# Branch products as seven products of quarters: what a two-block kernel's TensorE and its transfers make of it

## The chip, the cores and the metric

The kernel runs on one core of a Trainium2 chip. The metric is the device time of one execution in microseconds (us). Three runs of the kernel before took 1120.37, 1123.80 and 1120.04 us; their median is 1120.37.

## The reference

The input is one sequence of 512 tokens and 1024 features in float32. Two blocks follow each other. The first is a norm with modulation, a projection to 6144 columns, a pooling branch and a linear recurrence in chunks, and an output projection with a residual. The second has four branches of width 512 (a gated spatial mix, a sparse attention, a short convolution, an attention with forgetting), each with its own output product and its own gates, and these are what the change is about:

```python
h = rms_norm_2(x, norm_g)                      # 512 x 1024
proj = h @ w_in                                # its last 4096 columns are "gates"
ys = jnp.stack([y_a, y_b, y_c, y_d], axis=0)   # 4 x 512 tokens x 512
branch_d = jnp.einsum('nbsw,nwd->bsnd', ys, w_branch)      # 4 products 512x512 by 512x1024
g = jax.nn.sigmoid(gates.reshape(bsz, s, N_BRANCH, d))     # 4 products 512x1024 by 1024x1024
merged = jnp.sum(g * branch_d, axis=2)
return x + merged @ w_out                      # then a last norm
```

## The kernel before

**Products in three parts.** Every float32 operand is split into a high part and a rest, both in the fp32r format; `x w` is then high by high, high by rest and rest by high, three matmuls of 128x128 by 128x512. ScalarE copies the high part of a weight block into `whi` (L302), VectorE subtracts it for `wlo` (L303). There are three pairs of these buffers (WB) and splits run two products ahead (LA); `wget` hands out a pair and lets `pump` write the next ones. Activations are split by `split` (VectorE's line is L355), and one line, L329, issues every matmul.

**Weights.** The host lays all weights out as blocks ("raws") of 128 x 2048, 1024 KB, in the order in which they are used. SP loads them one after the other into a raw buffer as soon as one is free (`dma_raw`, L247; `used` frees one). There are three raw buffers; ahead of the gate stage three more are made, each of four 128x512 working tiles (`add_buf`). There are 54 working tiles ("slots") in all, which hold whatever else is live.

**The gate stage.** The branches come in the order 0, 2, 3, 1. Per branch the 512x1024 by 1024x1024 gate product is computed as seven products of quarters (`strassen_gate`, PRODUCTS), each of two items of 12 matmuls. The weights' quarters are combined where they lie: when a product's weights are split, `add_quarter` has POOL issue a transfer that adds the next quarter from DRAM to the one in the buffer (L261, ADDED: four sums of two halves of 512 KB per branch). Between and behind them stand the branch products (`wb_items`): for each half of the columns two loads of two row blocks, each by four blocks of 128 tokens, in three parts: 96 matmuls a branch. Their activations y (four tiles of 128x512 a branch) stay in slots from where a branch is computed. Their results are multiplied by the gate's sigmoid (L1769) and added to the sum over branches (L1774), both on VectorE:

```python
V.tensor_mul(s.f, s.f, hold["b"][t][:])
...
V.tensor_add(mg[t, hf].f, mg[t, hf].f, s.f)
```

`merged_T` then transposes the sum for the output product `w2`, which follows. What sets the order around the change: each engine runs its list as written by the items' order; SP's queue is in the order of the blocks, and POOL's in the order in which `add_quarter` is called.

**Other places that the change touches.** At the start, VectorE reduces the modulation's weights (`ttr`) in eight steps, each followed by 21 matmuls. In the first block `u_evac` builds window sums for the pooling by shift-and-add steps on POOL (L914), `spread` takes a squared tile, splits it and multiplies by a ones matrix to sum over partitions, `gate_item` reads the modulation's gate weights out of raw buffers (blocks `adg`), and `rstd` with `after1` and `norm_T` makes the two norms between the blocks (L1148, L1152, L1159). L1364 scales an attention's probabilities ahead of their transposes (L1395). XD keeps the residual in DRAM during the second block.

## Time and profile before

| | |
|---|---|
| median of three runs | 1120.37 us |
| the profiled execution's own time | 1121.16 us |
| its span, first to last instruction | 1119.4 us |
| mean granted TensorE clock | 0.998 |
| TensorE matmuls, busy | 1093.8 us, 98% of the span, 5189 |
| VectorE, ScalarE, POOL busy | 785.0, 636.8, 107.0 us |
| DMA | 139.54 MB, mean 125 GB/s |

The page comes from one execution. A busy time is the sum of an engine's instructions; matmuls are pipelined and their ends modelled, so the share of TensorE says that it rarely stands, not that it runs at its best. PEclk is the granted clock in parts of full speed (1.0 is 2.4 GHz, 0.5 is 1.2 GHz). The DMA share is the mean over the 16 DMA engines of the time that their packets took; as packets of one engine can lie over one another, a short stretch can read above 1. A chain of waits lists, going back from the last instruction, what each step had to wait for.

### The profile page before, as it was taken

Reading aid. Unit: us, or ns where it says so; the run is one execution under the profiler, and the core shown is the slowest. Engines: PE = TensorE matmul, PEld = TensorE weight load, DVE = VectorE, ACT = ScalarE, POOL = GpSimd, SP = SyncE. Lnnn points to the kernel's source line nnn. Section 1 sums busy time; section 2 is a strip of 40 time slices with the busy share of each in tenths; the row PEclk is TensorE's granted clock in tenths of the full one; section 3 lists DMA queues with packets and bytes.
Section 4 is the critical chain, followed back from the end, with each engine's and each line's share of the span. In section 5 each row is a group of like instructions: output and inputs, shape, how many; then the busy total and the mean of one; then the engine's idle time right before and its main releaser. Section 6 shows DMA issues by size and latency. Waiting matters only on the chain.

```text
span 1119.4 us, 14194 instructions
## 1 busy us (share of the span) xinstructions
PE 1093.8 (98%) x5189; PEld 904.7 (81%) x5189; DVE 785.0 (70%) x1586; ACT 636.8 (57%) x1025; POOL 107.0 (10%) x121
## 2 busy tenths in 40 slices
PE   6999999999999999999999999999999999999997
PEld 4788888888878888788887888888888888888885
DVE  7978788764779645889797846686655657565745
ACT  6595487955478464554246545754664554536513
POOL 1330210100520000000000000000111210122000
PEclk9999999999999999999999999999999999999999
DMA  9734223232222253232322222121586676768202
GB/s 326 285 132 164 80 92 135 76 113 76 76 76 76 96 203 116 95 113 104 122 76 76 85 85 81 71 76 57 169 207 177 173 205 160 188 151 220 101 1 75
DMA packets 39827, 139.54 MB, mean 125 GB/s; under 512 B 4551, under 2 KB 4807, under 8 KB 29901
## 3 DMA queue, kind: packets, MB, share of 16 engines
q1 hardware_dynamic: 32268, 120.81, 30.6%
q0 software_dynamic: 6912, 16.78, 8.7%
q10 hardware_dynamic: 576, 1.05, 0.3%
q8 instruction: 40, 0.66, 0.2%
q14 instruction: 31, 0.25, 0.1%
HBM read 134.42 MB, written 4.20 MB: 124 GB/s over the span
## 4 chain that ended last, share of the span: by engine, by line
PE 85%; DVE 5%; DMA 3%; ACT 3%; issue 2%; POOL 2%; SPq 0%; POOLq 0%; ACTq 0%
PE bank L329 83%; DMA slot<-in_adw_dram 2%; ACT slot L108 1%; PE bank L1395 1%; POOL slot L914 1%; ACT whi L302 1%; ACT L108 1%; POOL slot L913 1%; DMA raw<-in_wts_dram 1%; DVE slot L487 1%; DMA slot<-in_x_dram 1%; DVE slot L355 0%; DVE slot L1148 0%; DVE slot L1159 0%; DVE wlo L303 0%
## 5 line engine op out<-in xcount | busy, mean ns | idle before, releaser
L303 DVE TENSOR_TENSOR wlo<-raw,whi 128x1024 fp32r<-128x1024 f32 (+1 forms) x160 | 194.2, 1214 | 132.6 <-ACT whi L302 123.7
L302 ACT ACTIVATE whi<-raw 128x1024 fp32r<-128x1024 f32 (+1 forms) x160 | 168.1, 1051 | 202.2 <-PE bank L329 170.0
L329 PE MATMUL bank<-HH,whi 128*128 128x512 f32 x704 | 272.3, 397 | 2.4 <-ACT HH L108 2.1
L329 PE MATMUL bank<-HH,wlo 128*128 128x512 f32 x704 | 268.4, 391 | 0.0
L329 PE MATMUL bank<-HL,whi 128*128 128x512 f32 x704 | 267.3, 391 | 0.0
L329 PE MATMUL bank<-whi,slot 128*128 128x512 f32 x688 | 218.1, 392 | 0.0
L108 ACT ACTIVATE slot<-bank 128x512 f32<-128x512 f32 (+7 forms) x286 | 133.1, 495 | 55.5 <-PE bank L329 25.3
L108 ACT ACTIVATE slot<-slot 128x512 fp32r<-128x512 f32 (+4 forms) x199 | 112.3, 593 | 92.0 <-DVE slot L1930 19.2
L329 PEld LDWEIGHTS bank<-HH,whi 128*128 128x128 f32 x704 | 132.1, 188 | 31.8 <-ACT HH L108 5.5
L329 PEld LDWEIGHTS bank<-HH,wlo 128*128 128x128 f32 x704 | 132.5, 188 | 28.0
L329 PEld LDWEIGHTS bank<-HL,whi 128*128 128x128 f32 x704 | 132.6, 188 | 26.3
L329 PEld LDWEIGHTS bank<-whi,slot 128*128 128x128 f32 x688 | 129.1, 188 | 28.8 <-ACT slot L108 1.7
L329 PE MATMUL bank<-slot,slot 128*128 128x128 f32 (+5 forms) x754 | 132.4, 319 | 3.4 <-ACT slot L108 3.4
L329 PE MATMUL bank<-wlo,slot 128*128 128x512 f32 x336 | 130.9, 389 | 0.0
L329 PEld LDWEIGHTS bank<-slot,slot 128*128 128x128 f32 (+2 forms) x754 | 109.4, 186 | 18.2 <-issue 4.4
L108 ACT ACT_TABLE_LOAD x84 | 107.8, 1283 | 3.2 <-PEq L2069 0.7
L329 PE MATMUL bank<-whi,HH 128*128 128x512 f32 x248 | 97.8, 394 | 0.7 <-ACT slot L108 0.5
L329 PE MATMUL bank<-whi,HL 128*128 128x512 f32 x248 | 96.3, 391 | 1.3 <-DVE small L1152 1.3
L329 PE MATMUL bank<-wlo,HH 128*128 128x512 f32 x248 | 96.7, 390 | 0.0
L329 PEld LDWEIGHTS bank<-wlo,slot 128*128 128x128 f32 x336 | 63.1, 188 | 12.7
L261 POOL DMA_DIRECT2D slot<-in_wts_dram x28 | 24.5, 936 | 448.8 <-DMA slot<-in_wts_dram 395.7
L302 ACT ACTIVATE whi<-slot 128x512 fp32r<-128x512 f32 x61 | 38.5, 631 | 45.9 <-PE bank L329 35.2
(236 smaller groups left out, 1192.8 us busy)
## 6 DMA issues: line engine op xcount, KB each, us to landing
raw<-in_wts_dram SPq DMA_DIRECT2D x77, 1024.0 KB, 4.8
slot<-in_wts_dram SPq DMA_DIRECT2D x44, 256.0 KB, 4.8
slot<-in_adw_dram SPq DMA_DIRECT2D x32, 256.0 KB, 6.4
raw<-in_wts_dram POOLq DMA_DIRECT2D x16, 512.0 KB, 5.4
slot<-in_wts_dram POOLq DMA_DIRECT2D x28, 256.0 KB, 5.1
slot<-in_x_dram SPq DMA_DIRECT2D x16, 256.0 KB, 4.0
raw<-in_wts_dram SPq DMA_DIRECT2D x8, 448.0 KB, 5.8
slot<-in_rows_dram SPq DMA_DIRECT2D x11, 256.0 KB, 3.9
```

Source lines behind the costliest of these rows:

```text
L108: return A.activation(o, i, func, **kw)
L261: G.dma_start(b.at(c, w), wts[r_from, :, c:c + w], accum_op=ALU.add)
L302: A.activation(whi[s][:, c:c + n], b.at(o + c, n), AF.Copy)
L303: V.tensor_sub(wlo[s][:, c:c + n], b.at(o + c, n), whi[s][:, c:c + n])
L329: T.matmul(o, l, r, start=start, stop=stop, **kw)
L487: V.tensor_tensor_reduce(junk[i % 2].f, ada[k][i].f, cb[i % 2].f, 1.0, 0.0, ALU.mult, ALU.add, mds[k][:, i:i + 1])
L913: G.tensor_copy(d.f[:, 0:sh], src.f[:, 0:sh])
L914: G.tensor_add(d.f[:, sh:512], src.f[:, sh:512], src.f[:, 0:512 - sh])
L1395: T.transpose(tb[:, cs], P[u1].f[:, cs], IDENT)
```

## The change

**Branch products.** W of a branch (512 x 1024) and y (512 x 512) are cut into quarters, and seven products of quarters of 12 matmuls give what eight would: 84 matmuls a branch. The weights come in three blocks of two quarters, a, b and c, of 1024 KB each; four sums are added by transfers when the blocks have been loaded, a fifth after the third product has been split. Quarters b and c hold a second copy, so seven blocks a branch are loaded for gates and branch products where six were. The adds are no longer issued at once but put on a list (`later`) and issued two items later. The branch products now stand behind all seven gate products.

**y in DRAM.** Each tile of y is written to a DRAM tile YD when a branch has computed it (`keep`, 16 writes of 256 KB) and read back early in the branch's gate products (`y_steps`), where its quarters are split and its four sums formed by VectorE, one step with each item.

**Sums over branches.** In the second and third branch the sum over branches is done by transfers from slot to slot that add (16 of 256 KB), issued by POOL; in the last branch by VectorE.

**From the call's first try.** The gate weights `adg` are loaded into slots four items ahead; two constants are loaded by ScalarE's queue at the start; five more matmuls (WARM) stand behind the first transposes; one reduction goes earlier, copies and one scaling move between VectorE and ScalarE; pooling windows 8 and 16 take one running sum on VectorE and one subtraction; `spread` is handed a split made ahead; the norms multiply by rows that were scaled by -0.5 beforehand and have one VectorE step less; the transposes of the next tokens are written into the products of the current ones; the last norm writes into slots of its own.

```diff
-        pairs += [[f"B{n}_11"], [f"B{n}_21"], [f"B{n}_22"], [f"B{n}_12"], half(n, 1), half(n, 0)]
+        pairs += [[f"B{n}_11"], [f"B{n}_21"], [f"B{n}_22"], [f"B{n}_12"], [f"W{n}_a"], [f"W{n}_b"], [f"W{n}_c"]]
...
+PRODUCTS_W = ((1, "a", 0), (5, "b", 1), (6, "a", 1), (3, "c", 0), (7, "b", 0), (2, "c", 1), (4, "a", 1))
+ADDED_W = (("a", 1, "b", 0), ("b", 0, "c", 0), ("b", 1, "b", 0), ("a", 1, "a", 0))
...
     def dma_raw():
+        while ws["dma"] < len(raws) and raws[ws["dma"]][0][0].startswith("ad"):
+            ws["dma"] += 1
...
-        for o, r_from in to_add.pop(r, ()):
-            add_quarter(r, o, r_from)
+        for args in to_add.pop(r, ()):
+            later.append((ws["next"] + 2, args))
+        name = raws[r][0][0]
+        if name[0] == "W":
+            n = name[1]
+            later.extend((ws["next"] + 2, (r, h * 1024, quarter[f"{n}_{q}"], g * 1024))
+                         for t, h, q, g in ADDED_W if t == name[-1])
...
+            if name[0:2] == "W6":
+                add_quarter(r, o, quarter[f"{name[3]}_c"], 1024)
...
     def wget(name, ahead=LA):
+        while later and later[0][0] <= i:
+            add_quarter(*later.pop(0)[1])
         pump(i + ahead)
...
-    def spread(b, w, src, keep=False):
-        h, l = get(), get()
-        split(h.r, l.r, src.f)
+    def spread(b, w, hl):
+        h, l = hl
...
+            if w > 4:
+                on, d = get(), get()
+                G.memset(on.f, 1.0)
+                V.tensor_tensor_scan(d.f, on.f, u.f, 0.0, op0=ALU.mult, op1=ALU.add)
+                V.tensor_copy(on.f[:, 0:w], d.f[:, 0:w])
+                V.tensor_sub(on.f[:, w:512], d.f[:, w:512], d.f[:, 0:512 - w])
...
-        V.scalar_tensor_tensor(u, r, -0.5, r, op0=ALU.mult, op1=ALU.mult)
-        V.tensor_mul(u, u, v)
-        V.scalar_tensor_tensor(r, u, 1.5, r, op0=ALU.add, op1=ALU.mult)
+        V.scalar_tensor_tensor(u, r, v, r, op0=ALU.mult, op1=ALU.mult)
+        V.scalar_tensor_tensor(r, u, -3.0, r, op0=ALU.add, op1=ALU.mult)
...
+    def keep(n, k, slot):
+        nc.sync.dma_start(y_block(n, k), slot.f)
+        put(slot)
+        yb.add((n, k))
...
+    def y_steps(n):
+        def load():
+            for k in range(4):
+                y.append(get())
+                nc.sync.dma_start(y[k].f, y_block(n, k))
+        def plain(name, i, j):
+            def f():
+                h, l = q[name] = get(), get()
+                for k in range(2):
+                    dh, dl = (two(x).bitcast(F32R)[:, k] for x in (h, l))
+                    split(dh, dl, part(i, j, k))
...
+        return [load, None, None, plain(1, 0, 0), sums_, sum6, sum3, sum7, plain(2, 0, 1), plain(4, 1, 1), rest]
...
+    def wb_items(n):
+        def out(i, hf, part, banks_, free):
+            for t in range(2):
+                s = sg.pop((2 * i + t, hf))
+                b = banks_[t][:]
+                if part:
+                    u = part[t]
...
+                    else:
+                        V.tensor_sub(u.f, u.f, b)
+                    b = u.f
+                V.tensor_mul(s.f, s.f, b)
...
+                if last:
+                    V.tensor_add(mg[key].f, mg[key].f, s.f)
+                else:
+                    G.dma_start(mg[key].f, s.f, accum_op=ALU.add)
+                put(s)
+                for t in range(2):
+                    for k in range(2):
+                        mm(to[t][:], ah[:, k, ts_], h[:, c], opens and k == 0, False, **go)
+                        mm(to[t][:], ah[:, k, ts_], l[:, c], False, False, **go)
+                        mm(to[t][:], al[:, k, ts_], h[:, c], False, k == 1, **go)
+        items = [item(p) for p, _, _ in PRODUCTS_W]
+        if last:
+            items.insert(6, (None, lambda: merged_T(1, (0, 1)), None))
+            items.append((None, lambda: merged_T(1, (2, 3)), None))
...
-        for p, _ in PRODUCTS[0:6]:
+        for p, _ in PRODUCTS:
             r += product(p)
-        r += wb_items(n, 1)
-        a4 = product(4)
...
-        return r + a4 + wb_items(n, 0)
+        for i, f in enumerate(y_steps(n)):
+            if f:
+                r[i + 1] = both(f, r[i + 1])
+        return r + wb_items(n)
```

**POOL's queue in the gate stage, second branch.** A row is a transfer: its destination, its source and its size; 128x1024 is 512 KB. `in_wts_dram` rows add weights to a raw buffer or to slots that serve as one. Before:

```order
L261 DMA raw_113<-in_wts_dram 128x1024
L261 DMA slot_6499<-in_wts_dram 128x512
L261 DMA raw_113<-in_wts_dram 128x1024 x5
L261 DMA raw_114<-in_wts_dram 128x1024 x2
L261 DMA slot_6595<-in_wts_dram 128x512
L261 DMA slot_6596<-in_wts_dram 128x512
```

After, in the same place, with L1899 the sums over branches (L275 is the line of the weights' adds now):

```order
L275 DMA raw_114<-in_wts_dram 128x1024 x4
L275 DMA slot_6622<-in_wts_dram 128x512
L275 DMA slot_6623<-in_wts_dram 128x512
L275 DMA slot_6624<-in_wts_dram 128x512
L275 DMA slot_6625<-in_wts_dram 128x512
L1899 DMA slot_6771<-slot_7225 128x512
L275 DMA raw_113<-in_wts_dram 128x1024
L1899 DMA slot_6773<-slot_7227 128x512
L275 DMA slot_6533<-in_wts_dram 128x512
L275 DMA slot_6534<-in_wts_dram 128x512
L1899 DMA slot_6678<-slot_7132 128x512
L1899 DMA slot_6680<-slot_7134 128x512
```

The adds of weights for branch products have come in, and the sums over branches stand between them and the next branch's adds.

**VectorE at the branch products of the second branch.** `wlo` rows are weight splits; a row that reads a `bank` takes a matmul's result out of its accumulator. Before, L1769 multiplies by the gate and L1774 adds to the sum over branches:

```order
L1769 TENSOR_TENSOR slot_7104<-slot_7104,bank_65 128x512
L1769 TENSOR_TENSOR slot_7106<-slot_7106,bank_66 128x512
L1774 TENSOR_TENSOR slot_6706<-slot_6706,slot_7104 128x512
L1774 TENSOR_TENSOR slot_6708<-slot_6708,slot_7106 128x512
L303 TENSOR_TENSOR wlo_121<-slot_6554,whi_118 128x512
L1769 TENSOR_TENSOR slot_7035<-slot_7035,bank_64 128x512
```

After, L1883 combines two products and L1887 multiplies by the gate:

```order
L1883 TENSOR_TENSOR slot_7371<-bank_61,slot_7371 128x512
L1887 TENSOR_TENSOR slot_7225<-slot_7225,slot_7371 128x512
L317 TENSOR_TENSOR wlo_119<-slot_6624,whi_116 128x512
L1883 TENSOR_TENSOR span_7373<-bank_62,span_7373 128x512
L317 TENSOR_TENSOR wlo_119<-slot_6625,whi_116 128x512
L1887 TENSOR_TENSOR slot_7227<-slot_7227,span_7373 128x512
```

The additions have left VectorE's list in this branch, and combinations and more splits have come.

**SP's queue where the gate stage's loads begin.** A `raw` row of 128x2048 is one block; blocks in slots go in four rows. Before:

```order
L247 DMA raw_114<-in_wts_dram 128x2048
L247 DMA raw_115<-in_wts_dram 128x1024
L247 DMA raw_113<-in_wts_dram 128x2048
L247 DMA slot_6497<-in_wts_dram 128x512
L247 DMA span_6498<-in_wts_dram 128x512
L247 DMA raw_114<-in_wts_dram 128x2048
L247 DMA slot_6496<-in_wts_dram 128x512
```

After, with L1291 the writes of y and L1820 its reads:

```order
L1291 DMA YD<-slot_5829 128x512
L254 DMA raw_113<-in_wts_dram 128x2048
L1291 DMA YD<-slot_6012 128x512
L254 DMA raw_114<-in_wts_dram 128x1024
L254 DMA slot_6623<-in_wts_dram 128x512
L254 DMA slot_6624<-in_wts_dram 128x512
L254 DMA slot_6531<-in_wts_dram 128x512
L254 DMA raw_115<-in_wts_dram 128x2048
L1291 DMA YD<-slot_6098 128x512
L254 DMA slot_6532<-in_wts_dram 128x512
L1820 DMA slot_6555<-YD 128x512
L1820 DMA span_6553<-YD 128x512
```

The 128x1024 row is the last block of the projections in both. The writes and reads of y share the queue with the blocks.

## Rows read from the trace of the kernel before

**Rows 1.** The page's first part: span, busy time and share of each engine

```profile
span 1119.4 us, 14194 instructions
...
PE 1093.8 (98%) x5189; PEld 904.7 (81%) x5189; DVE 785.0 (70%) x1586; ACT 636.8 (57%) x1025; POOL 107.0 (10%) x121
```

**Rows 2.** Chain of waits, gate stage: start us, us, what, matmuls

```profile
850.35 60.41 PE bank L329 x264
...
1055.47 21.84 PE bank L329 x96
```

**Rows 3.** TensorE's timeline, first gate matmul: start us, us, what

```profile
822.58 0.39 PE L329 MATMUL bank<-whi,HH 128*128 128x512 f32 x1
```

**Rows 4.** TensorE's waits, whole span: us in total, times, longest

```profile
PE bank L1395 <- DVE slot L1364: 2.7, 1, 2.7
PE bank L329 <- DVE slot L355: 2.4, 3, 1.8
...
PE bank L329 <- DVE small L1152: 1.3, 1, 1.3
```

**Rows 5.** Windows: length, engines' busy us (count), PEclk, DMA share, GB/s

```profile
785.00:811.00 26.00, 26.00 (x123) 21.72 (x123) 16.74 (x37) 16.66 (x29) 2.80 (x3) 1.00 0.61 182
811.00:850.00 39.00, 38.99 (x177) 32.01 (x175) 22.42 (x28) 23.13 (x33) 6.01 (x7) 1.00 0.83 205
850.00:910.00 60.00, 59.99 (x264) 49.03 (x263) 34.21 (x46) 30.12 (x45) 12.13 (x14) 1.00 0.71 174
910.00:960.00 50.00, 49.99 (x220) 40.77 (x218) 33.90 (x47) 25.82 (x38) 5.21 (x6) 1.00 0.66 169
960.00:1014.00 54.00, 53.99 (x238) 44.37 (x238) 35.25 (x48) 25.90 (x38) 11.40 (x14) 1.00 0.69 176
1014.00:1042.00 28.00, 27.99 (x123) 22.47 (x122) 16.20 (x21) 16.55 (x25) 4.24 (x5) 1.00 1.00 278
1026.00:1034.00 8.00, 7.99 (x36) 6.22 (x35) 4.38 (x7) 4.56 (x7) 0.09 (x1) 1.00 1.08 251
20.00:40.00 20.00, 19.19 (x81) 14.60 (x80) 19.72 (x49) 10.59 (x15) 5.37 (x4) 1.00 1.04 391
```

**Rows 6.** The page's queues: packets, MB, share of 16 engines over the span

```profile
q1 hardware_dynamic: 32268, 120.81, 30.6%
q0 software_dynamic: 6912, 16.78, 8.7%
```

**Rows 7.** The same queues from 980 to 990 us

```profile
q0 software_dynamic: 560, 1.02, 64.1%
q1 hardware_dynamic: 195, 1.13, 32.8%
```

**Rows 8.** SP queue's timeline: the gate stage's first block is issued

```profile
784.97 0.33 SPq L247 DMA_DIRECT2D raw<-in_wts_dram  x1
```

**Rows 9.** TensorE's timeline in the first block, idle time before in brackets

```profile
324.31 1.08 PE L329 MATMUL bank<-slot,ONES 128*128 128x512 f32 x2 [1.75 <-DVE slot L355]
```

**Rows 10.** The window right behind it

```profile
325.00:329.00 4.00, 3.54 (x9) 2.60 (x10) 4.00 (x12) 2.36 (x4) 0.00 (x0) 0.57 0.00 0
```

**Rows 11.** Groups by form, whole span: busy us, mean ns, idle before

```profile
L685 DVE TENSOR_TENSOR_SCAN slot<-SCANM,slot 128x512 f32<-128x512 f32 x8 | 9.8, 1219 | 2.4 <-ACT slot L108 1.5 <-POOL slot L914 0.9
```

**Rows 12.** TensorE's timeline, two steps of the start

```profile
39.26 1.88 PE L329 MATMUL bank<-HH,whi 128*128 128x512 f32 x7
...
44.37 1.88 PE L329 MATMUL bank<-HH,whi 128*128 128x512 f32 x7
```

**Rows 13.** Groups by form from 811 to 1055 us

```profile
L303 DVE TENSOR_TENSOR wlo<-raw,whi 128x1024 fp32r<-128x1024 f32 x38 | 46.5, 1225 | 47.8 <-ACT whi L302 47.7
...
L1769 DVE TENSOR_TENSOR slot<-slot,bank 128x512 f32<-128x512 f32 x28 | 18.5, 681 | 2.1 <-PE bank L329 2.0
...
L261 POOL DMA_DIRECT2D raw<-in_wts_dram x16 | 13.8, 906 | 100.9 <-DVE wlo L303 66.0 <-DMA raw<-in_wts_dram 35.0
```

**Rows 14.** The page's DMA issues: count, KB each, us to landing

```profile
raw<-in_wts_dram POOLq DMA_DIRECT2D x16, 512.0 KB, 5.4
```

More of the change, by code (lines that the diff above doesn't have):

```diff
@@ L29 @@
 NSPAN = 2
+WARM = 5
 R1 = 1.5
@@ L57, in plan @@
 def plan():
-    def half(n, hf):
-        return [f"wb{n}_{hf}_{j}" for j in range(2)]
     raws = []
@@ L194 @@
                 if q == "12":
-                    for p, src in PRODUCTS[0:6]:
+                    for p, src in PRODUCTS:
                         flat += [(f"P{p}n{n}_{j}", f"{n}_{src}", j * 1024, 1024) for j in range(2)]
-            else:
-                if name[0:2] == "wb" and name[3:] == "_0_0":
-                    p, src = PRODUCTS[6]
-                    flat += [(f"P{p}n{name[2]}_{j}", f"{name[2]}_{src}", j * 1024, 1024) for j in range(2)]
+            elif name[0] == "W":
+                quarter[name[1:]] = r
+                n, q = name[1:].split("_")
+                if q == "c":
+                    flat += [(f"W{p}n{n}", f"{n}_{t}", h * 1024, 1024) for p, t, h in PRODUCTS_W]
+            else:
                 flat.append((name, r, o, w))
@@ L259, in add_quarter @@
         w = width(1024, b)
-        for c in range(o, o + 1024, w):
-            G.dma_start(b.at(c, w), wts[r_from, :, c:c + w], accum_op=ALU.add)
+        for c in range(0, 1024, w):
+            G.dma_start(b.at(o + c, w), wts[r_from, :, o_from + c:o_from + c + w], accum_op=ALU.add)
     def add_buf():
@@ L969, with both, mmf, gate_load @@
     gacc = {}
+    def both(first, item):
+        def mmf():
+            first()
+            item[1]()
+        return (item[0], mmf, item[2])
+    def gate_load(m, part):
+        def load():
+            r = flat[names.index(f"adg{m}{part}")][1]
+            gadw[m, part] = [get() for _ in range(4)]
+            for i, t in enumerate(gadw[m, part]):
+                nc.sync.dma_start(t.f, wts[r, :, i * 512:(i + 1) * 512])
+        return load
+    gadw = {}
     def gate_item(m, part):
         def mmf():
-            raw, r = adaget(f"adg{m}{part}")
+            adaget(f"adg{m}{part}")
             if part == "a":
@@ L976, in mmf @@
             acc = gacc[m]
-            acc_cols(acc.f, [raw[:, i * 512:(i + 1) * 512] for i in range(4)], 4 * "ab".index(part), 8)
-            used(r)
+            tiles = gadw.pop((m, part))
+            acc_cols(acc.f, [t.f for t in tiles], 4 * "ab".index(part), 8)
+            put(*tiles)
             if part == "a":
@@ L1136, in wout_final, with scale_row, rstd @@
             put(*src[k])
-    def rstd(t, scaled, row):
+    def scale_row(row):
+        for h in range(2):
+            act(row[h].f, row[h].f, AF.Copy, scale=-0.5)
+    def rstd(src, to, row):
         ss2, v, r, u = small(2), small(1), small(1), small(1)
@@ L1181, in norm_T @@
             dl = HL[:, 4 * h:4 * h + 4, t * 128:(t + 1) * 128]
-            split(dh, dl, b3)
+            with tc.high_priority():
+                split(dh, dl, b3)
             bput(b)
     presplit(mixH, range(8))
+    scale_row(ROW)
     wout_final("wh", mixH, after1)
@@ new lines, in y_steps, with part, two, load @@
+    def y_steps(n):
+        y, q = [], yq[n] = [], {}
+        def part(i, j, k):
+            return y[2 * j + k].f[:, 256 * i:256 * i + 256]
+        def two(s):
+            return s.f.rearrange("p (k t) -> p k t", t=256)
+        def load():
+            while any((n, k) not in yb for k in range(4)):
+                assert sides
+                step_sides(4)
+            for k in range(4):
[7 more added lines that the diff above has]
+                    split(dh, dl, part(i, j, k))
+            return f
+        def sums_():
+            q[5] = get()
+            for k in range(2):
+                V.tensor_sub(two(q[5])[:, k], part(1, 0, k), part(1, 1, k))
+        def sum6():
+            q[6] = get()
+            for k in range(2):
+                V.tensor_sub(two(q[6])[:, k], two(q[5])[:, k], part(0, 0, k))
+        def sum3():
+            q[3] = get()
+            for k in range(2):
+                V.tensor_add(two(q[3])[:, k], two(q[6])[:, k], part(0, 1, k))
+            q[5] = split_slot(q[5])
+        def sum7():
+            q[7] = get()
+            for k in range(2):
+                V.tensor_sub(two(q[7])[:, k], part(0, 0, k), part(1, 0, k))
+            q[6] = split_slot(q[6])
+        def rest():
+            put(*y)
+            q[3] = split_slot(q[3])
+            q[7] = split_slot(q[7])
+        return [load, None, None, plain(1, 0, 0), sums_, sum6, sum3, sum7, plain(2, 0, 1), plain(4, 1, 1), rest]
```

214 lines of the change are left out of this document (121 added, 93 removed).

## Prediction

> **What bounds the kernel now.** The page's first part has TensorE busy for 98% of a span of 1119.4 us [rows 1]. As the ends of its matmuls are modelled, I turned to the chain of waits. In the gate stage (gates and branch products) the chain is TensorE alone, piece joined to piece: 264 matmuls in 60.41 us, so 0.2288 us each [rows 2]. The stage's first matmul starts at 822.58 [rows 3]; its last is the 48th of the piece that begins at 1055.47, and 48 x 0.2275 us later it is 1066.4 [rows 2]. TensorE's list of waits comes third: no wait in it stands in the gate stage, and what there is elsewhere is a few us [rows 4].
>
> Then I looked at what this change loads more, the 16 DMA engines. In the gate stage they are busy for 0.66 to 1.00 of the time [rows 5], though TensorE never waits for them. The page's queues give prices. q1, the plain transfers, takes 30.6% of 1119.4 us for 120.81 MB, 2.835 us of all engines per MB; q0, the adding transfers, 8.7% for 16.78 MB, 5.80 us per MB [rows 6]. Two checks. From 785 to 1042 the shares times the lengths give 189 us [rows 5]; 32.0 MB of loads and 16.78 MB of adds by these prices give 188. And in ten microseconds where both queues run, q0 has 64.1% and q1 32.8% [rows 7]: together 0.97, so one takes its time from the other. The slack is 28%, no more.
>
> **The change, part by part.**
> 1. Branch products. Before, 2 halves x 2 loads x 2 x 4 row blocks x 3 = 96 matmuls a branch; now 7 products x 2 x 2 x 3 = 84. 48 fewer in all at 0.2288 us: -11.0 us of TensorE's chain.
> 2. What they cost the DMA engines. A quarter or block of 1024 KB is 1.049 MB, 2.97 us as a load; an add of half of it 3.04 us. The stage loads 7 blocks a branch instead of 6: 28 x 2.97 = 83.2 us. Adds of weights go from 8 to 13 a branch (8 for the gates as before, 4 when a, b and c are loaded, 1 after the third product): 52 x 3.04 = 158.1. Reading y back: 16 tiles of 0.262 MB at 0.74: 11.9. The sums over branches: 16 adding transfers from SBUF to SBUF, which the trace lacks. The nearest rows are a plain transfer, 0.74, and an add from DRAM, 1.52 [rows 6]; none excludes the low end, and they too read, add and write, so I take 1.52: 24.3 (low end 11.9). Sum 277.5 us, against 168.7 before (24 loads, 32 adds).
> 3. Which of it must be through before the stage ends. The last add is the one into block a between the third and the seventh product of the last branch, and 3.5 of the 4 blocks of the output weights are issued ahead of it: +10.4, so 288. What is done before the first gate matmul comes off. Before, the first load of the stage goes out at 784.97 [rows 8], and until 822.6 the engines do 26 x 0.61 + 11.6 x 0.83 = 25.5 us of work [rows 5]; all 37.6 us would be the most. The change issues two tiles earlier, and has six buffers as before: I take 30. 258 us are left.
> 4. How fast the engines can go. With work waiting they reached 1.00 over 28 us [rows 5]; 0.83 is the row for 811 to 850, with buffers full. A stretch can read above 1: 1.08 over 8 us, and 1.04 over 20 us at the start, 391 GB/s of plain transfers [rows 5], where 2.835 us per MB is 353. I take 0.97 (ends 0.88 and 1.05): 266 us. After the last add come its split, two products and transposes, some 7 us. The stage then ends at 822.6 + 266 + 7 = 1095.6, where before it ended at 1066.4: +29.2 us. TensorE alone would end it at 1055.4. So the 11.0 us are not seen: TensorE waits for splits, these for adds.
> 5. New waits. ScalarE's copies of y wait for its reload, issued three half-products ahead (8 us), and behind them on ScalarE stand the next weight splits; on the POOL queue the sums wait for VectorE's multiplies, and the next branch's adds stand behind them. Both are inside the 0.97 while the DMA engines are the limit. Where TensorE waits, its clock can drop: after 1.75 us of waiting [rows 9] the granted clock is 0.57 over 4 us, the lower of its two levels for most of them [rows 10]. That costs nothing more where a transfer sets the pace.
> 6. VectorE and ScalarE in the stage: seven splits of 1024 columns instead of four, three sums split besides y, six more combinations per branch; less eight additions in two branches. Hidden: VectorE is busy 34 of 60 us [rows 5].
> 7. The rest. Pooling windows 8 and 16 now take one VectorE scan (1.22 us [rows 11]) instead of three or four shift-and-add steps on POOL, and the ones-product's split is written ahead: the wait of rows 9 and the slow matmuls behind it, 3.3 us, may go; I take -2.5 (0 to -3.3). The norm after the first block has one VectorE step less and its transposes a tile ahead: -1 of the 1.5 us that the waits on L1152 and L355 there can cost [rows 4] (0 to -1.5). The wait on L1364 stays (0 to -2.7). At the start VectorE paces each of eight steps at 5.11 us [rows 12]; one reduction is moved ahead, one scaling moves off and two copies come on before the second step, so -0.5 (+1 to -1). The five extra matmuls stand in a wait. The end of the kernel: -0.2. Writing y during the projections costs nothing, the engines have room there. Sum -4.2 (+1 to -7).
>
> The profiled execution took 1121.2 us, 1.8 more than its span and 0.8 above the median of 1120.4. 1121.2 + 29.2 - 4.2 = 1146.
>
> The Trainium skill, "DMA: Bandwidth & Descriptors", section "Anatomy of one DMA — SWDGE (gpsimd) path", has a rule against this: a transfer from this queue costs about 2 us of fixed time and its bytes at 436 GB/s. By it (an estimate from the page) the stage's adds, 27.3 MB, would take 63 us of the engines instead of 158, the DMA engines would not be the limit, and the first rival would hold. The trace disagrees where it can be seen: 1.02 MB of adds in 6.41 us, 159 GB/s [rows 7].
>
> **The rivals.**
> - Transfers stay hidden. The adds' packets may in part be waiting, so that more of them at once go faster. For: TensorE never waited at a share of 1.00 for 28 us; 8 us read 1.08 and 20 us 1.04 [rows 5]. Against: rows 7, and the sum that came out at 188 of 189. It needs 258 us of work in the 226 that TensorE leaves, a rate of 1.14; or 1.09 with the sums at their low end. Then 1121.2 - 11.0 - 4.2 = 1106, faster.
> - VectorE sets the branch products. Per branch: seven splits at 1.225, six combinations and eight multiplies at 0.68 make 18.1 us [rows 13], in 84 x 0.2288 = 19.2 us; in the last branch eight additions bring 23.5, 4.3 us late; some 2 us of latency in each of the others. If transfers stay hidden: 1106 + 10 = 1116, no change. Against: the splits of the next gate product are few by then.
> - The POOL queue goes one by one. If each add waits until the one ahead has landed, 5.4 us [rows 14] and 0.9 of issue [rows 13], then 52 x 6.3 = 328 us; less 30, the stage ends at 1128 and the kernel at 1178. For: POOL holds them in one order, with waits on loads and multiplies between. Against: before, adds to different buffers overlap.
>
> **How the numbers follow.** Forecast 0.72, transfers hidden 0.15, VectorE 0.07, one by one 0.06. The forecast's own range: at a rate of 1.05 instead of 0.97 its 258 us take 246, the stage ends at 1075.6 and the kernel at 1126; with the cheap sums alone 246 us of work at 0.97 take 253, 1133; at 0.88, 293 us, 1173. The rest of item 7 moves it by 5 up and 3 down. The slow ends and the fast ones are not all met at once: 1120 to 1170. For 8 in 10 the low end must take in most of the near side: 1110, which leaves out the hidden case (0.15); above 1172 lies the one-by-one case, 0.06. A measurement of this kernel tells 0.5% from no change, 1114.8 to 1126.0. Faster: 0.15. Same: VectorE 0.07 and 0.02 of the forecast's near end. Slower: 0.70 of the forecast and 0.06, 0.76.
>
> **What would show it.** Right: in the gate stage a DMA share near 1.0 throughout, q0 with 31.5 MB and 16 to 17% of the span, TensorE waiting on VectorE's and ScalarE's splits and these on raw or slot tiles' transfers, gate stage about 273 us long, granted clock dips in it. The waits of rows 9 and on L1152 smaller. Wrong: a share that stays below 0.9 without waits of TensorE (then the prices do not add up, 1106); TensorE waiting on branch-sum multiplies with idle DMA engines (VectorE); or gaps in the DMA engines while POOL waits for its own transfers (one by one).

## The result: slower, by twice what was forecast

The changed kernel took 1177.95 us (median of four runs, 1177.18 to 1179.83) against 1122.09 us for the kernel before: a ratio of 1.050, 95% interval 1.0471 to 1.0529. The forecast was 1146 us, in a range of 1110 to 1172. The direction was right, the size was not: 56 us instead of 26.

The page of the profiled execution, its first part and its queues (columns as in [rows 1, 6]):

```profile
span 1178.0 us, 14451 instructions
...
PE 1106.9 (94%) x5151; PEld 906.3 (77%) x5151; DVE 823.5 (70%) x1666; ACT 671.2 (57%) x1089; POOL 121.7 (10%) x134
...
q1 hardware_dynamic: 40620, 133.30, 32.3%
q0 software_dynamic: 12816, 31.46, 14.9%
```

TensorE has 38 matmuls fewer and is 13 us longer busy. The adding queue moved the 31.46 MB that were forecast, in 175.5 us of the 16 DMA engines' time (14.9% of 1178.0) where the adds took 97.4 before [rows 6]. Below, "the engines" are these 16.

TensorE's timeline of the changed kernel, the first gate product:

```profile
815.22 0.39 PE L346 MATMUL bank<-whi,HH 128*128 128x512 f32 x1
```

It starts 7.4 us earlier than before [rows 3]. The loss lies behind it. Windows of the changed kernel, first the stretch ahead of the gate stage and the stage as a whole, then 30 us each (columns as in [rows 5]):

```profile
785.00:815.20 30.20, 29.41 (x142) 24.30 (x141) 16.82 (x36) 15.96 (x31) 5.25 (x6) 1.00 0.88 225
815.20:1121.00 305.80, 256.77 (x1029) 199.27 (x1027) 182.72 (x268) 156.14 (x243) 69.38 (x79) 0.92 0.84 203
...
850.00:880.00 30.00, 26.72 (x109) 21.59 (x110) 17.59 (x26) 17.17 (x27) 5.33 (x7) 0.94 0.69 190
880.00:910.00 30.00, 22.90 (x88) 17.46 (x87) 17.95 (x29) 12.06 (x20) 7.87 (x9) 0.89 1.01 213
910.00:940.00 30.00, 27.82 (x113) 22.11 (x114) 17.54 (x25) 17.76 (x28) 4.39 (x6) 0.94 0.67 179
940.00:970.00 30.00, 28.07 (x116) 22.48 (x115) 19.48 (x31) 12.21 (x21) 14.20 (x17) 0.94 1.03 252
970.00:1000.00 30.00, 22.01 (x80) 15.99 (x79) 17.26 (x26) 15.71 (x24) 5.94 (x7) 0.83 1.06 230
1000.00:1030.00 30.00, 29.41 (x129) 23.67 (x128) 19.65 (x29) 17.12 (x29) 9.13 (x12) 1.00 0.86 250
1030.00:1060.00 30.00, 15.92 (x61) 12.02 (x59) 11.47 (x19) 6.38 (x10) 12.95 (x15) 0.81 1.05 212
1060.00:1090.00 30.00, 26.58 (x101) 20.63 (x102) 19.69 (x28) 19.96 (x32) 2.60 (x3) 0.84 0.75 183
```

Read the last three columns. The DMA share swings: above 1.0 where a branch begins, 0.67 to 0.86 in the middle of one. In three of the four windows above 1.0 TensorE is busy for 16 to 23 of 30 us, at a granted clock below 0.9; in the fourth (940 to 970) it is busy for 28. Where the share is low TensorE runs, though in the last window still at a clock of 0.84, behind a long wait. Over the stage the share is 0.84. The matmuls themselves take longer too: 256.77 us for 1029, against 243.76 for 1074 in the stage before; at that pace they would have taken 233.5.

What TensorE waits for (whole span; us, times, longest), and below it ScalarE's and POOL's waits from 815 to 1125 us of the changed kernel:

```profile
PE bank L346 <- ACT whi L316: 31.1, 7, 8.5
PE bank L346 <- ACT slot L111: 9.1, 4, 3.7
PE bank L346 <- DVE wlo L317: 5.4, 12, 0.8
PE bank L1950 <- DVE slot L1897: 4.7, 3, 1.8
```

```profile
ACT whi L316 <- DMA raw<-in_wts_dram: 34.6, 10, 10.2
ACT slot L111 <- DMA slot<-slot: 29.8, 4, 14.0
...
ACT span L111 <- DMA slot<-span: 10.5, 2, 10.0
```

```profile
POOL slot L275 <- DMA slot<-in_wts_dram: 88.3, 12, 18.0
POOL raw L275 <- DVE wlo L317: 62.2, 11, 15.3
POOL raw L275 <- DMA raw<-in_wts_dram: 29.3, 4, 12.6
```

TensorE waits for the weights' splits; ScalarE, which writes these, waits for adds into its blocks (34.6 us) and for slots from which a sum over branches is still being read (40.3 us); and POOL waits 118 us for transfers of weights, because an add goes to a block whose load or last add has not landed. (In the kernel before POOL had 57 us of such waits, and TensorE none behind them.) Where this meets TensorE (its timeline, idle time in brackets) and POOL's queue (its timeline):

```profile
1041.44 0.80 PE L346 MATMUL bank<-whi,HH 128*128 128x512 f32 x1 [8.54 <-ACT whi L316]
...
1062.61 0.80 PE L346 MATMUL bank<-whi,slot 128*128 128x512 f32 x1 [7.69 <-ACT whi L316]
```

```profile
1050.69 0.87 POOL L275 DMA_DIRECT2D raw<-in_wts_dram  x1 [1.07 <-DVE wlo L317]
1064.12 0.86 POOL L275 DMA_DIRECT2D raw<-in_wts_dram  x1 [12.55 <-DMA raw<-in_wts_dram]
```

None of the long waits stands at a branch product: they are at the first three gate products of the next branch, whose weights also want their adds then. A matmul right after one takes 0.80 us instead of 0.39. So there were two readings. One: the engines have too much to do. Two: the work would fit, but what waits for it stands badly (slots on loan, adds behind adds).

### The profile page after: what moved, and what is told of

Same layout as the page of the kernel before. It is cut to its first block, busy times and chain, and to the rows that moved or that the text cites. A ratio compares the mean times of both kernels' runs of the same rounds, so it can differ in the third digit from the quotient of the medians.

```text
span 1178.0 us, 14451 instructions
## 1 busy us (share of the span) xinstructions
PE 1106.9 (94%) x5151; PEld 906.3 (77%) x5151; DVE 823.5 (70%) x1666; ACT 671.2 (57%) x1089; POOL 121.7 (10%) x134
## 3 DMA queue, kind: packets, MB, share of 16 engines
q0 software_dynamic: 12816, 31.46, 14.9%
## 4 chain that ended last, share of the span: by engine, by line
PE 62%; DMA 16%; DVE 11%; ACT 5%; issue 4%; POOL 1%; ACTq 0%; SPq 0%; DVEq 0%; POOLq 0%
PE bank L346 60%; DMA raw<-in_wts_dram 7%; DMA slot<-in_wts_dram 3%; DVE wlo L317 3%; DMA slot<-slot 2%; ACT slot L111 2%; ACT whi L316 2%; DMA slot<-in_adw_dram 2%; ACT L111 1%; DVE slot L482 1%; DVE slot L1411 1%; DMA YD<-slot 1%; DVE slot L372 1%; DVE best L1410 1%; PE bank L1459 1%
## 5 line engine op out<-in xcount | busy, mean ns | idle before, releaser
L317 DVE TENSOR_TENSOR wlo<-raw,whi 128x1024 fp32r<-128x1024 f32 (+1 forms) x173 | 210.0, 1215 | 169.7 <-ACT whi L316 158.6
L316 ACT ACTIVATE whi<-raw 128x1024 fp32r<-128x1024 f32 (+1 forms) x173 | 181.3, 1051 | 211.1 <-PE bank L346 150.5
L111 ACT ACTIVATE slot<-slot 128x512 fp32r<-128x512 f32 (+5 forms) x220 | 122.0, 580 | 108.6 <-DMA slot<-slot 29.8
L111 ACT ACTIVATE slot<-bank 128x512 f32<-128x512 f32 (+8 forms) x301 | 141.1, 499 | 66.2 <-PE bank L346 35.1
L346 PEld LDWEIGHTS bank<-slot,slot 128*128 128x128 f32 (+2 forms) x750 | 108.6, 186 | 18.2 <-issue 5.0
L346 PE MATMUL bank<-whi,HH 128*128 128x512 f32 x248 | 100.6, 406 | 17.7 <-ACT whi L316 10.2
L346 PE MATMUL bank<-wlo,HH 128*128 128x512 f32 x248 | 99.9, 403 | 1.3 <-DVE wlo L317 1.3
L275 POOL DMA_DIRECT2D slot<-in_wts_dram x42 | 39.9, 1079 | 484.3 <-DMA slot<-in_wts_dram 414.8
L346 PEld LDWEIGHTS bank<-whi,HH 128*128 128x128 f32 x248 | 48.3, 195 | 31.4 <-ACT whi L316 11.1
```

Of the source, the lines that this page charges most:

```text
L111: return A.activation(o, i, func, **kw)
L275: G.dma_start(b.at(o + c, w), wts[r_from, :, o_from + c:o_from + c + w], accum_op=ALU.add)
L316: A.activation(whi[s][:, c:c + n], b.at(o + c, n), AF.Copy)
L317: V.tensor_sub(wlo[s][:, c:c + n], b.at(o + c, n), whi[s][:, c:c + n])
L346: T.matmul(o, l, r, start=start, stop=stop, **kw)
```

## The experiments

Each is timed against the kernel before on the same chip. Differences below are between medians; the runs of one kernel lie 0.6 to 8 us apart, and the kernel before has medians of 1121.2 to 1122.4 us beside them.

**Sums over branches, e1 and e2.** e1 has VectorE add in all branches:

```diff
-                    G.dma_start(mg[key].f, s.f, accum_op=ALU.add)
+                    V.tensor_add(mg[key].f, mg[key].f, s.f)
```

> The changed kernel (1178 us) with the sums over branches added by VectorE in all branches, as in the last one: the 16 adding transfers between slots go, all else stays. Theory A (slots on loan: ScalarE's copies of y take slots whose sum has not yet left them, wait up to 14 us for it, 40 us in all, and the weight splits queue behind them): those waits go, TensorE's waits of 5 to 9 us behind them and the half-speed matmuls after each, so 35 to 45 us less, 1133 to 1143, and the granted clock above 0.985. Rival B (volume alone: the 16 DMA engines have too much to do): q0 falls from 31.5 to 27.3 MB, 17 us of the engines, so 17 to 21 us less, 1157 to 1161, with a DMA share that stays at 0.84 or above.

Measured: 1167.4 us, 10.6 less. Between nothing and either theory: less than A, less than B's own 17. e2 leaves the transfers and gives back their source slots later:

```diff
                     G.dma_start(mg[key].f, s.f, accum_op=ALU.add)
+                    held.append(s)
+                    continue
                 put(s)
...
+                    if p == 5 and j == 0 and held:
+                        put(*held)
+                        held.clear()
                     h, l = wget(f"P{p}n{n}_{j}")
```

> The changed kernel with the sums still made by transfers, but the slot that a sum is read from is given back only at the next branch's third product instead of at once; the same transfers, bytes and order of the queues. Theory A: ScalarE no longer waits for slot-to-slot transfers, so 20 to 40 us less, 1138 to 1158. Rival B: the volume is the same, so 1173 to 1181.

Measured: 1181.4 us, no gain. ScalarE's wait for slot-to-slot transfers fell from 40 to 15.5 us, and TensorE's wait for its splits stayed at 30.6. At the head of the last branch, though, ScalarE still stood at the same copies, now with no cause that the profile shows (its timeline in e2):

```profile
1049.32 0.72 ACT L111 ACTIVATE slot<-slot 128x256 fp32r<-128x256 f32 x2 [18.59 <-issue]
```

So e2 took away only part of these waits. Theory A's 35 to 45 us fall with e1, in which the transfers themselves are gone: 10.6 us are all that went with them. That another wait stands behind the one for the slot fits both runs, but is argued.

**The other edits alone, e3.** All hunks that have nothing to do with the branch products, applied to the kernel before.

> The kernel before with only the parts of the change that do not belong to the branch products (the start, pooling windows, ones-product split, gate weights into slots, norms, last norm). In the changed kernel's trace the first gate product starts 7.4 us earlier (815.2 against 822.6). If that is these parts' doing: 1120.4 - 7.4 - 0.2 = 1113 (1111 to 1115). If it is the y tiles that have left the slots: 1118 to 1121.

Measured: 1114.2 us, ratio 0.9932 (0.9917 to 0.9946). The 7.4 us are these edits' doing. This is also the fastest complete kernel of the study, faster than both.

**Work without waiters, e4 and e8b.** e4 adds transfers to the kernel before:

```diff
+            for h in range(3):
+                nc.sync.dma_start(JUNK[(3 * j + h) * 128:(3 * j + h + 1) * 128, :], wts[r, :, h % 2 * 1024:h % 2 * 1024 + 1024])
```

> The kernel before, with 72 transfers of 512 KB from DRAM to DRAM added in the gate stage (three behind each of its 24 blocks on SP's queue, 37.7 MB) that nothing waits for: about the DMA work that the change adds, with none of its waits. Rival B (volume): work of 189 + about 107 us at a rate of 0.84 to 1.0 does not fit into the stage's 244 us, so 20 to 60 us slower, 1140 to 1180. Theory A (waits): TensorE stays at its pace but for single late loads, 1120 to 1130.

Measured: 1121.7 us, the same, but it tells nothing. The window of its gate stage reads as that of the kernel before (share 0.67, 173 GB/s, in the same stretch):

```profile
822.60:1066.40 243.80, 243.76 (x1074) 198.99 (x1073) 153.50 (x207) 127.33 (x188) 36.51 (x42) 1.00 0.68 174
```

As nothing tied them, the transfers had been put into the queue early and ran in the first 270 us. e8b ties them to the stage: the source is a copy of gate tiles made there.

```diff
+    def traffic(s):
+        j = junk_i[0]
+        junk_i[0] += 1
+        nc.sync.dma_start(TD[j * 128:(j + 1) * 128, :], s.f)
+        if j % 2 and j > 2:
+            for _ in range(4):
+                k = junk_i[1]
+                junk_i[1] += 1
+                nc.sync.dma_start(JUNK[k * 256:(k + 1) * 256, :], TD[(j - 3) * 128:(j - 1) * 128, :])
```

> The kernel before, with transfers added that nothing waits for, this time tied to the gate stage: each sigmoid tile is also written to a DRAM scratch (32 of 256 KB), and from there 60 transfers of 512 KB go to other DRAM, on SP's queue; 39.8 MB, 113 us of the engines by q1's price, about the work that the change adds. If the volume alone makes gate adds and loads late: work of 168.7 + 113 + 8 us against a stage of 244, so 15 us (at a rate of 1.0) to 60 us (at 0.84) slower, 1136 to 1180. If it is the order in POOL's queue (adds for the branch products, which wait for blocks just called for and for one another, stand ahead of the gate's adds): 1120 to 1128.

Measured: 1150.9 us, 28.5 more. Three of its windows:

```profile
850.00:880.00 30.00, 29.99 (x133) 24.51 (x132) 16.04 (x22) 13.91 (x22) 4.35 (x5) 1.00 1.02 314
...
970.00:1000.00 30.00, 25.45 (x99) 19.83 (x98) 11.37 (x14) 11.71 (x17) 1.72 (x2) 0.89 1.01 307
...
1060.00:1090.00 30.00, 28.43 (x133) 23.16 (x132) 20.57 (x31) 16.34 (x28) 0.00 (x0) 1.00 1.01 359
```

Here the engines stay near 1.0 all through the stage (0.94 to 1.05 in eight such windows). The gate's adds landed after 10.3 us instead of 5.4 [rows 14] (the page's DMA issues; KB each, us to landing):

```profile
raw<-in_wts_dram POOLq DMA_DIRECT2D x16, 512.0 KB, 10.3
```

But this is not the price of the work alone, since something does wait for these transfers: VectorE multiplies into the very gate tile that an added transfer copies out, and may write it only once the transfer has read it. VectorE's waits from 812 to 1100 us, then one of them and TensorE's wait right behind it (timelines):

```profile
DVE slot L1772 <- DMA TD<-slot: 23.1, 6, 8.9
```

```profile
1031.23 0.69 DVE L1772 TENSOR_TENSOR slot<-slot,bank 128x512 f32<-128x512 f32 x1 [8.86 <-DMA TD<-slot]
```

```profile
1033.11 0.80 PE L332 MATMUL bank<-wlo,HH 128*128 128x512 f32 x1 [5.64 <-DVE wlo L306]
```

TensorE's waits on VectorE's splits, 11.2 us in all, stand almost wholly behind two such waits. How much of the 28.5 us is the work, and how much this, e8b does not show.

**Without the adds of weights, e5 and e6.** Both drop the `later.extend` of ADDED_W and the add after W6; e6 also has e1's edit.

> The changed kernel without its 20 adds of weights for the branch products (the branch products are then computed from blocks that were not summed; the adds for the gates stay). 10.5 MB of adding transfers go, 61 us of the engines by the price before. Theory C (the engines are swamped at the head of a branch, where gate adds, sums, loads and y meet: share 1.0 to 1.1 there, while the gate products wait for their adds): those stretches shorten, TensorE's waits of 5 to 9 us go for the most part, 1120 to 1140. Rival D (the sums alone, which stand in the same queue, hold up the gate adds): 1160 to 1175, since e1 already took all that the sums cost.

> As e5, and the sums over branches on VectorE as in e1: POOL's queue then holds the same adds as the kernel before, while SP still loads 28 blocks and reads y back (95 us of the engines instead of 71). Theory C: TensorE runs through the gate stage but for a wait or two, 1103 to 1112. If the loads and y cost by themselves, or the splits of y on ScalarE and VectorE: 1115 to 1130.

Measured: e5 1146.5 us, 31.4 less than the changed kernel, between the two theories and nearer to C; e6 1125.0. So the adds cost 42.4 us beside VectorE's sums (e1 against e6), and the sums by transfer 21.5 us without the adds (e5 against e6). e6 is no faster than the kernel before, though TensorE has 11 us less to do: measured against what TensorE's work would give (1103, as worked out at the head of the next section), something of the new products costs 22 us with no adds of theirs at all. The second branch has next to no part in it, TensorE runs through it (a window in it, e6, with 251 matmuls):

```profile
875.50:933.50 58.00, 57.64 (x251) 46.59 (x250) 44.18 (x66) 36.38 (x56) 6.55 (x8) 1.00 0.72 192
```

**When and where the adds are issued, e7 and e8.** e7 takes the `+ 2` out of both places where `later` is filled.

> The changed kernel with the adds put into POOL's queue at the moment at which their block is called for, not two items later; the same bytes. If the late call is what makes adds land late (5.4 us a landing before, 8 now, against some 11 us between a block's first and third product): 10 to 25 us less, 1153 to 1168. Theory C: the engines have the same to do in the same stretches, 1172 to 1184; or slower, where adds for a block that is not loaded yet hold the queue.

Measured: 1180.8 us, no gain. e8 adds in POOL's own arithmetic:

```diff
+    def sum_here(n, t, h, q, g):
+        to, src = raw_b[quarter[f"{n}_{t}"]], raw_b[quarter[f"{n}_{q}"]]
+        w = width(1024, to, src)
+        for c in range(0, 1024, w):
+            G.tensor_add(to.at(h * 1024 + c, w), to.at(h * 1024 + c, w), src.at(g * 1024 + c, w))
```

> The changed kernel with the branch products' weights added by POOL itself in its tiles (24 to 40 additions of 128x512 or 128x1024, at 1.1 us per 512 columns by the additions of the kernel before, some 11 us a branch) and the sums over branches by VectorE: no adding transfers but those for the gates. Theory C: as e6 if POOL's additions beside VectorE cost nothing, 1103 to 1115; by what POOL takes from VectorE and by its own waits for blocks, which stand ahead of the next branch's gate adds, up to 1140.

Measured: 1156.5 us, 10.9 less than e1 and far from e6. POOL's additions took 1.5 to 1.9 us per 512 columns here, where those of the kernel before took 1.14 (groups by form, of e8 in the stage and of the kernel before):

```profile
L271 POOL TENSOR_TENSOR slot<-slot,slot 128x512 f32<-128x512 f32 x22 | 40.4, 1867 | 29.9 <-DVE wlo L327 18.9 <-DMA slot<-in_wts_dram 9.7 <-DMA slot<-YD 1.1
```

```profile
L914 POOL TENSOR_TENSOR slot<-slot 128x511 f32<-128x511 f32 x8 | 9.1, 1140 | 0.0
```

VectorE paid too. Its multiplications of two slots took 1.12 us instead of 0.68 (the same line of the program in e8 and in e1), and with the same 1682 instructions as in e1 it was busy for 862.7 us instead of 832.0. VectorE and POOL are both slower side by side, so e8 does not tell what the adds' transfers cost.

```profile
L1897 DVE TENSOR_TENSOR slot<-slot,slot 128x512 f32<-128x512 f32 x20 | 22.1, 1117 | 0.1
```

```profile
L1887 DVE TENSOR_TENSOR slot<-slot,slot 128x512 f32<-128x512 f32 x20 | 13.4, 683 | 0.1
```

**The order in POOL's queue, e9 to e12.** e9 calls the branch products' adds 12 items later; e10 does that with e1's edit.

```diff
+DUE = {("b", 1, "b"): 1, ("a", 1, "b"): 0, ("a", 1, "a"): 3, ("b", 0, "c"): 4}
...
+                    due = names.index(f"P6n{n}_0") + DUE[t, h, q]
+                    later.append((max(due, ws["next"] + 2), (r, h * 1024, quarter[f"{n}_{q}"], g * 1024)))
```

> The changed kernel with the same adds, bytes and sums, in another order: the four adds for a branch's products are put into POOL's queue behind that branch's last gate add (at its fifth gate product and after, some 12 items later than before and two to six items ahead of their use) instead of at the head of the branch, between the gate's first adds. Order theory (POOL's queue held up at the head of a branch): 20 to 40 us less, 1138 to 1158. Volume theory: 1172 to 1184.

> As e9, and the sums over branches on VectorE as in e1. Order theory: nothing but gate adds is left at the head of a branch, so as the kernel without these adds and with VectorE's sums (1125) and up to 15 more where the late adds are now late for their own products: 1125 to 1140. Volume theory: as e1, 1160 to 1170.

Measured: 1177.5 and 1164.3 us, the same as the changed kernel and as e1 (1167.4). That was no test: in POOL's queue the adds for the second branch's block a still stood ahead of the gate's (four transfers to slots, at this place in the changed kernel and in e9):

```profile
877.29 3.54 POOL L275 DMA_DIRECT2D slot<-in_wts_dram  x4 [9.07 <-DMA slot<-in_wts_dram]
```

```profile
873.48 3.54 POOL L279 DMA_DIRECT2D slot<-in_wts_dram  x4 [9.34 <-DMA slot<-in_wts_dram]
```

So POOL's queue does not simply follow the order of the calls of `add_quarter`, as was said ahead of the prediction. e11 and e12 make the adds depend on a gate tile (for 16 of the 20 adds, by 28 added VectorE steps, not 64: 1694 against 1666 instructions):

```diff
+            if tie:
+                x = b.at(o + c, w)[:, 0:1]
+                V.scalar_tensor_tensor(x, sg[tie].f[:, 0:1], 0.0, x, op0=ALU.mult, op1=ALU.add)
             G.dma_start(b.at(o + c, w), ...
```

> The changed kernel with the same adds and sums, and 64 one-column VectorE steps that change no value but make each add for a branch product wait for a gate tile of the same branch, so that these adds really stand behind the gate's first adds in POOL's queue (in e9 the queue's order came out as in the changed kernel: adds go into it when their block is there, whatever the order of the calls). Order theory: the gate's adds for the third product go out at once, TensorE's waits of 5 to 9 us at the first products of a branch shrink, 15 to 35 us less, 1143 to 1163. If the rest of the loss is not the order but the sheer work (rate 1.0 would still leave some 29 us against the kernel before): not below 1140. No change, 1172 to 1184, if order has no part in it.

> As e11, and the sums over branches on VectorE. Order theory: 17 us of the engines less than e11 and no slots on loan at the head of a branch, 1125 to 1145. No part of the order: as e1, 1160 to 1170.

Measured: e11 1176.2 us, e12 1155.0. With the sums by transfer the order alone changes nothing that can be told: TensorE's waits became shorter and more (e11, 812 to 1130 us; the changed kernel has 31.1, 7, 8.5), and some now stand at the branch products.

```profile
PE bank L356 <- ACT whi L326: 22.1, 11, 5.2
PE bank L356 <- ACT slot L112: 6.9, 3, 5.9
PE bank L356 <- DVE wlo L327: 6.1, 15, 0.8
```

With VectorE's sums it gains 12.4 us on e1. Two of e12's windows, whose shares are 0.69 and 0.67 in the changed kernel and 0.77 and 0.73 in e1:

```profile
850.00:880.00 30.00, 23.96 (x99) 18.54 (x100) 14.70 (x24) 14.68 (x27) 6.21 (x8) 0.99 0.97 221
...
910.00:940.00 30.00, 25.17 (x100) 19.41 (x99) 13.73 (x22) 16.31 (x27) 5.26 (x6) 0.94 0.82 199
```

The engines are more evenly full now, and it is still 34 us slower than the kernel before.

**Work or waits, e13.** e6 with e8b's transfers, two for four.

> The kernel of e6 (no adds of weights for the branch products, so their blocks are not summed; sums on VectorE; 1125 us) with as much DMA work as those adds make put back as transfers that nothing waits for: 32 writes of 256 KB and 30 transfers of 512 KB on SP's queue, 24.1 MB, some 65 us of the engines at the 2.7 us per MB that e8b shows. Between e6 and e1 (1167), which differ by these adds alone, lie 42 us. If that is the work: 1155 to 1170. If it is what waits for the adds (splits for their block, POOL's queue for one add after another): 1128 to 1142.

Measured: 1153.8 us, 28.7 more than e6. Here the gate tiles are used much later, and the compute engines together waited 1.7 us for the added transfers. Two things keep 28.7 from being the price of the work alone. More was put back than had been taken out: 68 us of the engines (39.0% of 1153.7 against 34.0% of 1123.2) where the adds have 58 (e1's and e6's q0, 13.1% of 1165.9 against 8.4% of 1123.2). And the added writes stand in SP's queue, which waited for their gate tiles with loads behind them (SP's waits in e13, 812 to 1110 us):

```profile
SPq L1960 <- ACT slot L111: 82.2, 28, 14.8
```

So of the 42.4 us between e6 and e1 some 28.7 are the work, and rather less; what SP's waits have in that is not shown. e12, where the same adds stand well in POOL's queue, comes out at the same time as this kernel (1155.0), 30.0 more than e6.

**The end of the stage, e14.** e6 without the eight `V.tensor_add` of the last branch.

> The kernel of e6 without the eight additions of the last branch to the sum (its share is left out of the output). In e6 VectorE is busy 19.7 of the last 20 us of the branch products, and the last two products take 12.5 us instead of 5.4. If VectorE sets that tail: 8 x 0.7 = 5 to 8 us less, 1117 to 1120. If it is the latency of product, multiply and transpose: 1122 to 1126.

Measured: 1118.5 us, 6.6 less, as the first reading had it. The last 20 us of the branch products in e6 and, at a place 6 us earlier, in e14:

```profile
1050.00:1070.00 20.00, 13.08 (x52) 8.85 (x51) 19.71 (x32) 9.10 (x15) 0.00 (x0) 0.83 0.16 52
```

```profile
1044.00:1064.00 20.00, 15.99 (x72) 12.74 (x71) 18.51 (x28) 11.79 (x20) 0.00 (x0) 0.93 0.34 111
```

But without these additions the transposes of the sum no longer wait for the last branch's products either: their waits for VectorE, 4.0 us in e6, are gone in e14, and so e14 takes out part of the latency together with the work. For VectorE's work speaks that it is busy for 19.7 and 18.5 of the 20 us, and that in e14 too TensorE waits for one of its steps:

```profile
1060.27 0.50 PE L340 MATMUL bank<-whi,slot 128*128 128x512 f32 x1 [4.01 <-DVE slot L1875]
```

Against it speaks the kernel before: VectorE is busy for 18.2 of the last 20 us there, and TensorE for all 20.

## Why the prediction was too low, step by step

The runs can be set in a row: 1114.2 (e3), less 11.0 of TensorE's work, is 1103.2, which no run measured. The new products without adds cost 21.8 on top (e6; 6.6 of it the last branch's additions), their adds 42.4 (e6 to e1), the sums by transfer 10.6 (e1 to the changed kernel). That is 1178.0. It adds up by construction, and another order of the steps would give other parts. Of the 42.4, some 28.7 and rather less are the adds' work (e13), some 13.6 and rather more their place and the waits for them (e13 to e1).

1. *TensorE's 11.0 us.* Real but never seen: in e6's second branch 251 matmuls stand in a window of 58.0 us, and at 0.2288 each they would take 57.4.
2. *The work of the engines.* Right (only the slack is 26% by its own rows, 189 of 257 us, not 28%). 277.5 + 10.4 = 288 us were forecast; the shares of the first two windows above give 30.2 x 0.88 + 305.8 x 0.84 = 283. The sums, for which there was no row, were taken as adds from DRAM at 24.3 us: between e1 (13.1% of 1165.9) and the changed kernel (14.9% of 1178.0) lie 22.8. The adds' price held too: leaving out 10.49 MB freed 56.7 us in e5 (14.9% of 1178.0 less 10.4% of 1142.6), 5.4 us per MB. The Trainium skill, "DMA: Bandwidth & Descriptors", section "Anatomy of one DMA — SWDGE (gpsimd) path", has a transfer's bytes move at 436 GB/s; by that (an estimate from the page) it would have been 24. The 56.7 us measured here disagree.
3. *Work into time.* Not shown either way: 29.2 us were forecast for it, and e8b, with about as much work added (107 us of the engines), is 28.5 slower. That looks like a hit, but VectorE's waits for the added writes are in the 28.5, so the agreement may be luck.
4. *The rate of 0.97.* This is the step that failed. It was read from stretches of the kernel before that had transfers in plenty, and the engines can go that fast: where more work was always queued, in e8b from 822.6 to 1096 us, their share was 0.98. In the changed kernel it was 0.84 over the stage, below the low end of 0.88, for which 1173 had been worked out; 258 us of work at 0.84 are 307 us instead of 266, and the stage took 305.8 us instead of some 273. The engines were not slower, they were not asked evenly: 0.67 to 0.86 in the middle of a branch, and at the next one's head adds, loads, sums and y at once. Why they were not asked is only read from the trace. SP's loads wait for blocks that splits must first set free (last two fences of this section), but the kernel before waited as long for that, 174.5 us; new are the 42.9 us in which loads into slots waited for activations' splits (L372), where it had 1.1. No run tried more blocks or more slots.
5. *New waits "inside the 0.97".* Failed with it. What waits was named rightly (ScalarE's copies of y with weight splits behind them, adds behind sums on POOL), but it was priced at nothing. The place of the adds and the waits for them cost 12 to 14 us, rather more (e12, e13) and the sums 11 to 21, their work included (e1, e5 and e6). "That costs nothing more where a transfer sets the pace", said of the clock, was not tested; the stage's matmuls took 23 us more in all, at granted clocks down to 0.81 in a window.
6. *VectorE "hidden".* Probably wrong at the end: 34 busy of 60 us is an average over a branch, and the last 20 us had 19.7 in e6. The rival had 4.3 us there; the eight additions are worth 6.6 (e14), in which the transposes' wait for them is included.
7. *The rest.* Forecast -4.2, low end -7 (its parts' ends add up to -8.7); measured -7.4 in e3, against 1121.6 on the same chip. The first product after the first block starts 5.4 us earlier (449.05 against 454.40), where the ones-product and the norm had been taken at 3.5; the start itself came out 0.5 us later (its steps stand at 39.74 and 44.86, [rows 12] at 39.26 and 44.37), not earlier.

The rivals: transfers do not stay hidden (without the adds and the sums by transfer, e6, 52.9 us go). "One by one" had given 1178 and looks like a hit, but its mechanism is not it: in the stage POOL issued 79 transfers, and only some 20 of them waited for another transfer. e11 does not settle it: its waits for weights fell from 118 to 40 us, but 53 came on the new ties, and the time stayed. VectorE is a part, not the limit.

What stays open: 15 of the 22 us that e6 loses against TensorE's pace are not taken apart (candidates are ScalarE's and VectorE's splits of y, the half-speed matmuls, and the latency of the last two products), nor are the 6.6 us of e14 divided between VectorE's work and that latency. Nor is it shown why the sums by transfer cost 21.5 us alone and 10.6 beside the adds; both make the same stretches full, so a part of either may be had only once. And how the 42.4 us of the adds divide into work and waits is known only roughly.

SP's waits in the gate stage of the changed kernel, for step 4:

```profile
SPq L254 <- DVE wlo L317: 171.4, 57, 23.7
SPq L254 <- DVE slot L372: 42.9, 3, 21.4
```

and in that of the kernel before (822 to 1067 us):

```profile
SPq L247 <- DVE wlo L303: 174.5, 46, 17.1
```

## What to carry to other kernels

When a change puts transfers in place of matmuls, sum the transfers' work by their own measured price, but do not turn it into time by the best rate seen: that rate holds where work is always queued. Price the stretch where loads, adds and reads meet by itself. A resource busy for two thirds of a stage on average can be full where it counts. An experiment on the order of transfers has to be read back from the queue first: in e9 the calls moved by some 12 items and the queue's first two branches did not. And before traffic counts as work that nobody waits for, ask the trace who waited for it: in e8b it was VectorE, for 23.1 us.

## What the runs showed of the hardware

An add from slot to slot costs the DMA engines as much as one from DRAM: 22.8 us for 4.19 MB, 5.4 us per MB, twice a plain transfer. Plain copies from DRAM to DRAM cost 2.9 us per MB (e4: 40.4% of 1119.4 us for 158.56 MB, against 30.6% of 1119.4 for 120.81). POOL's additions ran at 1.5 to 1.9 us per 512 columns beside a busy VectorE in the gate stage, 1.14 in the first block, and beside them VectorE's multiplications of two slots took 1.12 us instead of 0.68 (e8 against e1).
